# One planned order for scan, attention and gates of a gated mixer block, and a causal mask moved from TensorE to VectorE

## The chip, the cores and the metric

The kernel runs on one core of one Trainium2 chip. The metric is the device time of one execution in microseconds (us); lower is better. A core has a matrix engine (TensorE, in a profile PE, with its weight loads shown apart as PEld), a vector engine (VectorE, DVE), a scalar engine (ScalarE, ACT), a general engine (GpSimd, POOL) and a queue engine (SyncE, SP). Each works off its own list of instructions in order, and they wait for each other through semaphores.

## The reference

One layer of a streaming encoder on 512 tokens of width 1024: a half-step feed-forward, a mixer with two branches, and a second half-step feed-forward. The change lies in the mixer.

```python
h = rms_norm(x, mix_norm);  p = h @ w_in     # RWKV columns | FoX q, k, v, forget logits | gates A, B
y_A = rwkv7_mixer(token_shift(p_rwkv))       # 8 heads x 64, state S_t = S w_t + (S a_t) b_t' + v_t k_t'
y_B = forgetting_attention(q, k, v, log_f)   # 8 heads x 64, causal
x = x + (sigmoid(g_A) * y_A @ P_A + sigmoid(g_B) * y_B @ P_B) @ w_out

def one_block(i, q_i, c_i):                  # forgetting attention, 128 queries at a time
    s = einsum('bhqd,bhkd->bhqk', q_i, k) * scale + c_i[..., :, None] - cum[..., None, :]
    s = where(pos_k <= pos_q, s, -inf)       # the causal mask
    pr = softmax(s, axis=-1)
    return einsum('bhqk,bhkd->bhqd', pr, v)
```

## The kernel before

All activations lie transposed, 128 features on the partitions and 512 tokens along them. Products of weights and activations are made in three matmuls of split operands (`mm3`, lines 143 to 145): high by high, high by low, low by high. ScalarE rounds the high part of a weight column block (`whi`), VectorE subtracts it from the raw block (`wlo`), and eight groups of three matmuls then use it.

The stretch that the change touches begins when the first two pairs of attention heads have their queries and keys. Four kinds of work run beside each other in it:

- **The scan.** The recurrence of the first branch is worked in 16 chunks of 32 tokens (loop over `c`, lines 1522 to 1556). In each chunk TensorE makes `xps` (L1529), VectorE copies it to `Xs` (L1532), TensorE makes `ups` (L1536), ScalarE copies that into the chunk's operand `RD` with four copies (L1538, L1539), TensorE makes `sps` (the next state, L1544) and `yps` (the output, L1548), VectorE scales the state into the next chunk's `RD` with two instructions (L1551), and ScalarE copies the output (L1556). Each step waits for the one before it. Every second chunk, `stage` transposes the values and keys of two chunks (`vp`, `bp`, L1506 and L1509), and ScalarE copies them.
- **The attention.** Four pairs of heads, and in each three groups of query blocks: (0, 1), (2,), (3,). For each of the two heads `q`, TensorE writes logits into a bank `lp` with two matmuls for each query block (L1600, L1601), and a third adds the mask: the identity times `dmask`, which holds 0 and -1e30 (L1602, bf16, 128 by 128, on the diagonal block alone). VectorE takes the negated maximum (L1608), ScalarE the exponential with its sum (L1609), VectorE the reciprocal and the division (L1611, L1614), TensorE transposes (L1618), ScalarE copies (L1620), TensorE multiplies with the values (L1632), VectorE copies the result out (L1634).
- **The last key rows.** Query and key columns of head pairs 2 and 3 (`load_qk`): 24 matmuls each, and a norm of each row.
- **The gates.** Nine blocks of gate columns (`early`), 24 matmuls each, a product with the row norm (L1331), a tanh (L1334) and a store to memory.

What sets the order: each engine's list is written by a scheduler in the compiling layer, which goes by its own estimate of times, and the kernel ties places down with `tc.issue_after`. The list `holes` (line 1553) says after which scan step each group of three weight matmuls may stand: two groups behind `xps`, two behind `ups`, two or three behind `yps`. `AHEAD` (line 1560) says from which chunk on a head pair's operands are split. A class `Queued` can make an engine keep the order in which the source calls it (`written(True)`); it is on just before this stretch and again behind it, and off within it. The stores of the gates go out on SP's queue, between the loads of weights.

Of the kernel before, what the change touches and what calls it, by code (L numbers as in the profile page):

```python
# [18 lines left out]
P = 128  # L19
T = 512  # L20
# [30 lines left out]
def kernel(  # L51
# [67 lines left out]
    dmask = cp.tile([P, P], BF16, name="dmask")  # L119
# [50 lines left out]


# [222 lines left out]
    def masks():  # L394
# [7 lines left out]
        pool.affine_select(out=dmask[:], in_=dmask[:], compare_op=ALU.is_ge, fill=-1e30, base=0,  # L402
# [617 lines left out]
    with ExitStack() as mx:  # L1020
        rp = mx.enter_context(tc.tile_pool(name="rp", bufs=1))
        holes = []
# [303 lines left out]
        def gate(c0, m, g):  # L1326
            ps = bank("pgt")
            mms = mix.cols(ps[:], *load_w(win(c0 + m * P), KD, P), P, holes)

            def out(whole=True):  # L1330
                dve.tensor_tensor(g, ps[:], mix.rstd[:], op=ALU.mult)  # L1331
                if whole:
                    with tc.issue_after(qks["last"].ins):
                        qks["tanh"] = act.activation(g, g, AF.Tanh, scale=0.5)  # L1334
            return mms[-1], out


        def early(n):
            m = n + NP + 3
            g = xp.tile([P, T], F32, tag="acc", name="gs", bufs=2)  # L1340
            mm, scaled = gate(COL_GA, m, g[:])

            def out(whole=True):
                scaled(whole)
                if whole:
                    nc.sync.dma_start(gsave[m], g[:])
            return mm, out, g[:]


        class Rows(Columns):  # L1350
# [11 lines left out]
            def load(s, holes=()):  # L1362
                s.weights()
                mix.cols(s.ps[:], *s.w, P, holes)
# [35 lines left out]

        def load_qk(p, holes=()):
            rows = [Rows(p, n) for n in range(2)]
            for r in rows:
                r.load(holes)
                r.out()
            for r in rows:
                each([r], "square", "high", "sum")
            for r in rows:
                each([r], "log", "root", "scale")
            qks[p] = [r.o for r in rows]  # L1410
# [69 lines left out]
        each((b1,), "log", "root")  # L1480
        gate_out(True)
        last = dve.last
        written(False)
        with tc.issue_after(last.ins):
            b1.scale()
# [14 lines left out]
        def stage(c, behind=None):  # L1500
            late = ExitStack()
            if behind:
                late.enter_context(tc.issue_after(behind.ins))
# [18 lines left out]
        for c in range(NC):  # L1522
# [31 lines left out]
            if c % 2 == 0 and c + 2 < NC:  # L1554
                stage(c + 2, hy)
# [387 lines left out]
```

## Time and profile before

| what | us |
|---|---|
| median of three runs | 1104.52 (1104.48 to 1104.61) |
| the profiled execution | 1104.68 |
| its span, first to last instruction | 1103.0 |
| TensorE busy in the span | 1093.4 |
| the stretch of scan and attention | about 517 to 670 of the span |

A page of the profile gives busy time and counts by engine, the span in slices, the chain of work that ended last, and groups of instructions. A row of the timeline reads: start, duration, engine, line, operation, what is written `<-` what is read, shapes, how many; in brackets the idle time before it and what ended it. Matmuls overlap, so the pitch of a matmul, the start of the next minus its own start, is what it takes of TensorE's time; its shown duration is longer. The shown count of a matmul with plain 32-bit operands is twice that of the program.

### The profile page before, as it was taken

What the parts mean: (1) busy time and instruction counts of PE and PEld (TensorE: products, weight loads), DVE (VectorE), ACT (ScalarE), POOL (GpSimd) and SP (SyncE); (2) the same over time, 40 slices, a digit from 0 to 9 for tenths busy, and PEclk for the clock granted to TensorE, in tenths of its full rate; (3) what the DMA queues carried; (4) which work ended last, traced back from release to release, by engine and by line L of the source; (5) the groups of instructions that cost most, each with busy time, mean ns of one, the idle gap of its engine ahead of it and who ended that gap; (6) DMA issues with size and microseconds to landing.
All of it is one profiled execution on the core that took longest, in us unless ns stands there. A gap on an engine that the chain in (4) does not pass through costs nothing.

```text
span 1103.0 us, 16226 instructions
## 1 busy us (share of the span) xinstructions
PE 1093.4 (99%) x6082; PEld 893.1 (81%) x6082; DVE 837.1 (76%) x1130; ACT 670.4 (61%) x1046; POOL 207.0 (19%) x247
## 2 busy tenths in 40 slices
PE   9999999999999999999999999999999999999997
PEld 7888888888887888887777787888888888888886
DVE  7997676789766699788666667877697756789874
ACT  6765556675555756346787666633586555576554
POOL 1211211133204111401000011112311202115210
PEclk9999999999999999999999999999999999999999
DMA  8989887889926334445113234544968888869982
GB/s 226 249 176 236 195 181 190 192 153 193 241 77 195 94 104 117 115 134 139 45 40 96 86 100 144 175 135 141 285 153 190 195 215 172 183 159 204 236 189 77
DMA packets 140236, 177.09 MB, mean 161 GB/s; under 512 B 9726, under 2 KB 75838, under 8 KB 140158
## 3 DMA queue, kind: packets, MB, share of 16 engines
q0 software_dynamic: 32688, 68.30, 33.0%
q1 hardware_dynamic: 106734, 106.31, 31.4%
q10 hardware_dynamic: 736, 1.45, 0.3%
q8 instruction: 48, 0.79, 0.3%
q14 instruction: 30, 0.25, 0.1%
HBM read 163.51 MB, written 12.52 MB: 160 GB/s over the span
## 4 chain that ended last, share of the span: by engine, by line
PE 97%; ACT 1%; DMA 1%; DVE 1%; issue 0%; DVEq 0%; ACTq 0%
PE P L71 39%; PE P L143 5%; PE P L144 5%; PE P L145 5%; PE pgt L143 3%; PE pgt L145 2%; PE pgt L144 2%; PE pk L145 2%; PE pk L143 2%; PE pk L144 2%; PE ppj L71 2%; PE pb L71 1%; PE pa L71 1%; PE pq L143 1%; PE pw L144 1%; PE pw L143 1%
## 5 line engine op out<-in xcount | busy, mean ns | idle before, releaser
L135 ACT CAST whi<-raw 128x1024 fp32r<-128x1024 f32 (+3 forms) x57 | 55.3, 970 | 64.8 <-issue 19.3
L71 PE MATMUL P<-sraw,q 128*128 128x512 f32 x344 | 91.3, 389 | 0.0
L136 DVE TENSOR_TENSOR wlo<-raw,whi 128x1024 fp32r<-128x1024 f32 (+3 forms) x58 | 66.1, 1140 | 19.5 <-ACT whi L135 18.2
L71 PEld LDWEIGHTS P<-sraw,q 128*128 128x128 f32 x344 | 64.6, 188 | 13.4
L71 PE MATMUL P<-swhi,q 128*128 128x512 f32 x224 | 71.4, 390 | 0.0
L71 PE MATMUL P<-sraw,wxh 128*128 128x512 f32 x200 | 68.4, 394 | 0.0
L71 PE MATMUL P<-swhi,wxh 128*128 128x512 f32 x144 | 56.9, 395 | 0.0
L71 PE MATMUL P<-swhi,wxl 128*128 128x512 f32 x144 | 56.1, 390 | 0.0
L71 PE MATMUL P<-swlo,wxh 128*128 128x512 f32 x144 | 56.1, 389 | 0.0
L71 PE MATMUL P<-sraw,wxl 128*128 128x512 f32 x136 | 53.0, 390 | 0.0
L633 POOL DMA_DIRECT2D cb<-in_ffn_w_dram x20 | 24.1, 1203 | 149.6 <-DVE cd L71 85.2
L143 PE MATMUL pgt<-xh,whi 128*128 128x512 f32 x120 | 50.5, 421 | 0.0
L633 POOL DMA_DIRECT2D cd<-in_ffn_w_dram x24 | 29.5, 1230 | 104.2 <-DVE swlo L71 38.6
L71 PEld LDWEIGHTS P<-swhi,q 128*128 128x128 f32 x224 | 42.0, 188 | 8.7
L144 PE MATMUL pgt<-xl,whi 128*128 128x512 f32 x120 | 47.2, 393 | 0.0
L145 PE MATMUL pgt<-xh,wlo 128*128 128x512 f32 x120 | 47.1, 392 | 0.0
L71 PE MATMUL P<-swlo,q 128*128 128x512 f32 x112 | 43.6, 389 | 0.0
L71 PEld LDWEIGHTS P<-sraw,wxh 128*128 128x128 f32 x200 | 37.2, 188 | 7.3
L71 ACT CAST sraw<-cd 128x1024 fp32r<-128x1024 f32 x30 | 31.5, 1051 | 15.0 <-PE P L71 11.5
L71 DVE TENSOR_TENSOR swlo<-ca,swhi 128x1024 fp32r<-128x1024 f32 x24 | 29.2, 1222 | 14.0 <-ACT swhi L71 14.0
L71 DVE TENSOR_TENSOR swlo<-cc,swhi 128x1024 fp32r<-128x1024 f32 x20 | 24.5, 1225 | 18.9 <-ACT swhi L71 18.5
L71 DVE TENSOR_TENSOR u<-P,u 128x512 f32<-128x512 f32 x52 | 34.1, 684 | 5.8 <-ACT u L71 5.7
(624 smaller groups left out, 3371.3 us busy)
## 6 DMA issues: line engine op xcount, KB each, us to landing
raw<-in_w_in_dram SPq DMA_DIRECT2D x40, 512.0 KB
cc<-in_ffn_w_dram SPq DMA_DIRECT2D x36, 512.0 KB
cb<-in_ffn_w_dram POOLq DMA_DIRECT2D x36, 512.0 KB, 6.1
cb<-in_ffn_w_dram SPq DMA_DIRECT2D x32, 512.0 KB
cd<-in_ffn_w_dram POOLq DMA_DIRECT2D x32, 512.0 KB, 7.6
ca<-in_ffn_w_dram POOLq DMA_DIRECT2D x32, 512.0 KB, 7.2
ca<-in_ffn_w_dram SPq DMA_DIRECT2D x20, 512.0 KB
cd<-in_ffn_w_dram SPq DMA_DIRECT2D x18, 512.0 KB
```

What stands on the lines that cost most here:

```text
L71: q.last = do(*a, **kw)
L135: (hi_eng or act).copy(hi[:], raw[:])
L136: (eng or dve).tensor_tensor(lo[:], raw[:], hi[:].bitcast(F32), op=ALU.subtract)
L143: pe.matmul(ps, whi, xhi, start=first, stop=False, skip_group_check=onto)
L144: pe.matmul(ps, whi, xlo, start=False, stop=False, skip_group_check=onto)
L145: return pe.matmul(ps, wlo, xhi, start=False, stop=last, skip_group_check=onto)
L633: nc.gpsimd.dma_start(to, s.block(b, n, h), accum_op=ALU.add)
```

## The change

Everything of the stretch is entered into a `Plan`: an operation has an engine, a time in us, what it waits for, a rank, and the buffers it takes and frees. The plan then runs a clock of its own and always takes the operation that can start first, the lower rank first among equals; before an operation of rank over 0 on VectorE or ScalarE it looks whether a scan step could start within 1.32 times the operation's time, and takes that instead. It calls the operations in this order with the `Queued` wrapper on, so the written order is the order on TensorE, ScalarE and VectorE. `holes`, `AHEAD` and the waits between steps are gone. The wrapper stays on through the work behind the stretch, where its restart is dropped. The stores of these gates go out on POOL's queue. `dmask` grows to 128 by 512, with the mask in its last 128 columns, and is no operand of TensorE any more: VectorE adds it to the logits in the instruction that takes the maximum. The other splits, products and copies are the same.

```diff
-    dmask = cp.tile([P, P], BF16, name="dmask")
+    dmask = cp.tile([P, T], BF16, name="dmask")
...
+    class Plan:
...
+        def start(s, o):
+            to, now = o["engine"], s.idle.get(o["engine"], 0.0)
+            for d in o["deps"]:
+                if d["end"] is None:
+                    return None
+                by = d["engine"]
+                lag = 0.28 if by == "PE" else 0.15 if by == to else 0.2
+                now = max(now, d["end"] + (0.0 if by == to == "PE" else lag + 0.66 * (to == "PE")))
+            for name in set(o["takes"]):
...
+        def run(s):
+            todo = list(s.ops)
+            while todo:
+                at = {n: now for n, o in enumerate(todo) for now in [s.start(o)] if now is not None}
+                n = min(at, key=lambda n: (at[n], todo[n]["rank"], n))
+                o = todo[n]
+                if o["engine"] in ("DVE", "ACT") and o["rank"] > 0:
+                    until = at[n] + 1.32 * o["us"]
+                    n = next((m for m in at if todo[m]["engine"] == o["engine"] and todo[m]["rank"] == 0
+                              and at[m] < until), n)
...
+        SCAN, SIDE, NEXT, ROWS, FILL = range(5)
...
-            holes += [hx, hx, hu, hu, hy, hy] + [hy] * (c >= NC // 2)
...
+            e = op("PE", 0.58, on(product_x, c), *staged[c], *states.get(c, [begin]), rank=SCAN, takes=["pr"])
+            e = op("DVE", 0.22, copy_x, e, rank=SCAN, takes=["Xs"], frees=["pr"])
+            e = op("PE", 0.6, on(product_u, c), e, rank=SCAN, takes=["pr"], frees=["Xs"])
+            e = op("ACT", 1.07, on(copy_u, c), e, rank=SCAN, frees=["pr"])
...
-        AHEAD = (1, 6, 9, 12)
...
-                        pe.matmul(l, qb[q][:, bs], klc[q][:, 0:n], start=False, stop=False)
-                        pe.matmul(l[:, b * P:n], identb[:], dmask[:], start=False, stop=True)
+                    pe.matmul(l, qb[q][:, bs], klc[q][:, 0:n], start=False, stop=True)
...
-                        dve.tensor_reduce(mb, l, axis=AX.X, op=ALU.max, negate=True)
-                        act.activation(pt[:, at[b]:at[b] + n], l, AF.Exp, bias=mb, accum_out=mx[:, NB + b:NB + b + 1])
+                dve.tensor_tensor_reduce(l, l, dmask[:, T - (b + 1) * P:T], -1.0, 3e38, op0=ALU.add, op1=ALU.min,
+                                         accum_out=top)
...
+                act.activation(pts[:, q, n], s.lp[q][:, n], AF.Exp, bias=top, scale=-1.0, accum_out=sum_)
...
-                    nc.sync.dma_start(gsave[m], g[:])
+                nc.gpsimd.dma_start(gsave[m], g.t[:])
...
-        written(True)
-        pe.last, act.last, dve.last = gate_mm, filled, yl3
```

In the built program the new instruction on VectorE is two: one (`ISA lp,mx<-lp,dmask`) that adds, negates, writes the bank back and keeps the smallest value, and one (`ISA mx`) that writes this value out. TensorE's list behind the stretch is the same as before, row by row.

On TensorE, the first logits of head pair 2 (`kb`, `qa` and `klc`, `qb` are the split keys and queries, `RD` the scan's operands, `vp` and `bp` the scan's transposes) stood like this before:

```order
2620 L1600 MATMUL lp<-kb_5573,qa_5571 128x128
2621 L1601 MATMUL lp<-klc_3933,qb_4975 128x128
2622 L1602 LDWEIGHTS identb
2623 L1602 MATMUL lp<-dmask,identb 128x128
2624 L1600 MATMUL lp<-kb_5573,qa_5571 128x256
2625 L1601 MATMUL lp<-klc_3933,qb_4975 128x256
2626 L1602 LDWEIGHTS identb
2627 L1602 MATMUL lp<-dmask,identb 128x128
2628 L1544 MATMUL sps<-RD_4163,RD_4165 64x64 x8
```

and stand like this now:

```order
2470 L71 MATMUL vp<-ident,V_2815 64x128 x4
2471 L71 MATMUL lp<-kb_4959,qa_4957 128x128
2472 L71 MATMUL lp<-klc_3933,qb_4183 128x128
2473 L71 MATMUL lp<-kb_4959,qa_4957 128x256
2474 L71 MATMUL lp<-klc_3933,qb_4183 128x256
2475 L71 MATMUL lp<-kb_4959,qa_4957 128x384
2476 L71 MATMUL lp<-klc_3933,qb_4183 128x384
2477 L71 MATMUL bp<-ident,BK_2546 128x128
```

The two mask matmuls are gone, the next query block of the same head follows at once, and the group stands between the scan's transposes, about three chunks earlier in the scan than before (behind `sps` of chunk 6; before, ahead of `sps` of chunk 9).

On VectorE, between the state of one chunk and the `Xs` copy of the next (`pts` are the exponentials, `mx` the maxima and sums, `gs` a gate), chunk 7 stood like this before:

```order
589 L1551 TENSOR_TENSOR RD_4164<-sps,PC 64x4x64 x2
590 L136 TENSOR_TENSOR wlo<-raw,whi 128x1024
591 L1611 RECIPROCAL mx_4996<-mx_4996 128x1
592 L1532 COPY Xs<-xps 128x128
593 L1614 TENSOR_SCALAR pts<-pts,mx_4996 128x512
```

and chunk 4 stands like this now:

```order
586 L71 TENSOR_TENSOR RD_4156<-sps,PC 64x4x64 x2
587 L71 ISA lp,mx_4652<-lp,dmask 128x128
588 L71 ISA mx_4652 128x1
589 L71 ISA lp,mx_4652<-lp,dmask 128x256
590 L71 ISA mx_4652 128x1
591 L71 TENSOR_TENSOR wlo<-raw,whi 128x1024
592 L71 COPY Xs<-xps 128x128
```

In both a weight split stands right ahead of the scan's copy; now two masked maxima stand ahead of that. Such a split stands right ahead of `Xs` in five of the 16 chunks now (1, 4, 6, 13 and 14).

More of the change, by code (lines that the diff above doesn't have):

```diff
@@ L1399, in each @@
                     getattr(r, name)()
[L1401 to L1410, printed above, removed]
         qks = {}
@@ L1526, with product_x @@
+        def product_x(c):
+            Y["x"] = xps = pr.tile([P, 2, 64], F32, tag="b", name="xps")
             for p, q in heads()[::-1]:
                 o = (p // 2) * 64 + q * C
[L1528 to L1532 removed]
```

411 lines of the change are left out of this document (271 added, 140 removed).

## Prediction

> **What bounds the kernel now.** I read the page first, then one window over the stretch, then who waited for whom on TensorE there, then single rows of the timeline.
>
> ```profile
> span 1103.0 us, 16226 instructions
> PE 1093.4 (99%) x6082; PEld 893.1 (81%) x6082; DVE 837.1 (76%) x1130; ACT 670.4 (61%) x1046; POOL 207.0 (19%) x247
> PE 97%; ACT 1%; DMA 1%; DVE 1%; issue 0%; DVEq 0%; ACTq 0%
> ```
>
> The chain that ends last is TensorE for 97% of the span, so time is won or lost where TensorE does less, or waits more. The window over the stretch (columns: busy time and count by engine):
>
> ```profile
> 517.10:670.00 152.90, 151.76 (x1599) 117.91 (x1598) 104.00 (x230) 111.23 (x284) 7.86 (x15) 1.00 0.28 80
> ```
>
> TensorE is busy for 151.76 of 152.90 us; VectorE stands idle for 48.9 us of it and ScalarE for 41.7. All that TensorE waited there is 1.14 us, in three waits (waiter, releaser, total, times, longest):
>
> ```profile
> PE sps L1544 <- ACT RD L1539: 0.6, 1, 0.6
> PE lp L1618 <- DVE pts L1614: 0.3, 1, 0.3
> PE xps L1529 <- DVE RD L1551: 0.2, 1, 0.2
> ```
>
> So the order before leaves little to gain: a better order can give back 1.14 us here and no more. What is left to gain is work that TensorE no longer does.
>
> **Part 1: the mask leaves TensorE.** There are 32 of these matmuls:
>
> ```profile
> L1602 PE MATMUL lp<-dmask,identb x32: 229/229/233, 529.8 to 657.4; 128*128 128x128 bf16 x32
> ```
>
> Their price is a pitch, from one start to the next, and not the 229 ns of the row. Timeline of TensorE at the first logits of pair 2, at a mask followed by a weight matmul, and at a mask followed by the scan:
>
> ```profile
> 603.64 0.23 PE L1602 MATMUL lp<-dmask,identb 128*128 128x128 bf16 x1
> 603.68 0.36 PE L1600 MATMUL lp<-kb,qa 128*128 128x256 f32 x1
> 603.88 0.28 PE L1601 MATMUL lp<-klc,qb 128*128 128x256 f32 x1
> 604.00 0.23 PE L1602 MATMUL lp<-dmask,identb 128*128 128x128 bf16 x1
> 604.86 0.69 PE L1544 MATMUL sps<-RD,RD 128*64 128x64 f32 x16 [0.63 <-ACT RD L1539]
> ...
> 569.33 0.23 PE L1602 MATMUL lp<-dmask,identb 128*128 128x128 bf16 x1
> 569.37 0.48 PE L144 MATMUL pgt<-xl,whi 128*128 128x512 f32 x1
> 569.68 0.40 PE L145 MATMUL pgt<-xh,wlo 128*128 128x512 f32 x1
> 569.91 0.39 PE L143 MATMUL pgt<-xh,whi 128*128 128x512 f32 x1
> ...
> 635.81 0.23 PE L1602 MATMUL lp<-dmask,identb 128*128 128x128 bf16 x1
> 635.97 0.69 PE L1544 MATMUL sps<-RD,RD 128*64 128x64 f32 x16
> ```
>
> The mask itself takes 0.04 (603.64 to 603.68). The matmul of split operands behind it takes 0.08 more than its like: 0.20 (603.68 to 603.88) where the next one of the same width takes 0.12, and 0.31 (569.37 to 569.68) where a weight matmul takes 0.23 (569.68 to 569.91). In the order before, 14 masks have such a matmul behind them, 12 a scan or value product, 6 a transpose. Ahead of the scan a mask takes 0.16, but this 0.12 is no gain: a plain step into the scan has nearly the same toll, as these rows show, 0.32 (622.85 to 623.17) against 0.23 going in, and 0.34 (623.56 to 623.90) coming out.
>
> ```profile
> 622.85 0.40 PE L145 MATMUL pgt<-xh,wlo 128*128 128x512 f32 x1
> 623.17 0.46 PE L1536 MATMUL ups<-Xs,Tall 64*64 64x64 f32 x8
> 623.56 0.50 PE L143 MATMUL pgt<-xh,whi 128*128 128x512 f32 x1
> 623.90 0.40 PE L144 MATMUL pgt<-xl,whi 128*128 128x512 f32 x1
> ```
>
> Sum: 32 x 0.04 + 14 x 0.08 = 1.28 + 1.12 = 2.4 us less. The floor is the bare pitch, 1.3; the ceiling, with 0.05 for each of eight 128-wide matmuls ahead of a mask that might run closer to their width, 2.8. I take 2.4, since both of its terms stand in rows.
>
> **Part 2: the order.** The same products stand on TensorE in both kernels, so order costs only through tolls and waits. Tolls: counted in the two orders, narrow plain products are entered from weights, masks or transposes 52 times before and 54 times now (0.09 each), and left toward split-operand matmuls 42 and 34 times (0.11), toward transposes 10 and 20 times (about half as dear): 0.2 for the entries, 0.9 against the exits, 0.5 for the transposes. That is zero to within 0.2 us.
>
> Waits: 1.14 us could go. The longest, 0.63 at 604.86, came because ScalarE made a weight high part ahead of the scan's copies:
>
> ```profile
> 602.67 1.05 ACT L135 CAST whi<-raw 128x1024 fp32r<-128x1024 f32 x1
> 603.74 0.25 ACT L1538 COPY RD<-ups 32x128 f32<-32x128 f32 x1
> ```
>
> The plan's rule (a scan step goes first if it could start within 1.32 operations) is aimed at this, and behind every `ups` TensorE now has over 2.0 us of other work by the pitches above; the copies need 0.3 and then 1.06. What could be late next is the other side: behind `xps` the cover falls from at least 1.58 before to 0.9 to 1.0 in two chunks (11 and 14). How much the copy of `xps` needs when VectorE is free or busy is seen in chunk 7:
>
> ```profile
> 577.92 0.45 PE L1529 MATMUL xps<-RD,G 128*32 128x64 f32 x16 [0.20 <-DVE RD L1551]
> 578.29 0.50 PE L143 MATMUL pgt<-xh,whi 128*128 128x512 f32 x1
> 579.89 0.45 PE L1536 MATMUL ups<-Xs,Tall 64*64 64x64 f32 x8
> ...
> 577.80 1.22 DVE L136 TENSOR_TENSOR wlo<-raw,whi 128x1024 fp32r<-128x1024 f32 x1
> 578.94 0.15 DVE L1611 RECIPROCAL mx<-mx 128x1 f32<-128x1 f32 x1
> 579.13 0.29 DVE L1532 COPY Xs<-xps 128x128 f32<-128x128 f32 x1
> ```
>
> Behind a weight split the copy began 0.84 after the next matmul's start at 578.29 and `ups` followed 0.47 after its end: 1.60 in all, with a cover of 1.60 and no wait that the profile shows. With VectorE free some 0.75 less is needed. I take half of the 1.14 as gained, 0.6: between 1.1 gained and, if the thin covers fail (below), 1.0 lost.
>
> The operands' splits, the transposes of chunk 0 (which move into the stretch from weight matmuls just ahead of it, where TensorE did not wait either), and the stores on POOL's queue I cost at nothing. What hides the stores: a store is wanted only when its buffer is used again two gates later, over 10 us. Behind them on POOL stand the loads of gates for the last products; 33 weight matmuls (33 x 0.23 = 7.6 us) now end the stretch, which cover them.
>
> **Part 3: the mask on VectorE.** 32 maxima, and each gets a second input, a written bank and a second instruction that reads its result out. The rows of before (busy, mean ns), and the nearest ones for two inputs:
>
> ```profile
> L1608 DVE TENSOR_REDUCE mx<-lp 128x1 f32<-128x512 f32 x8 | 5.4, 688 | 3.2 <-PE lp L1602 3.0
> L1608 DVE TENSOR_REDUCE mx<-lp 128x1 f32<-128x384 f32 x8 | 4.3, 555 | 5.0 <-PE lp L1602 5.0
> L1608 DVE TENSOR_REDUCE mx<-lp 128x1 f32<-128x256 f32 x8 | 3.4, 423 | 1.5 <-ACT pts L1609 1.3
> L1608 DVE TENSOR_REDUCE mx<-lp 128x1 f32<-128x128 f32 x8 | 2.3, 284 | 0.6 <-PE lp L1602 0.6
> L1331 DVE TENSOR_TENSOR gs<-pgt,rstd 128x512 f32<-128x512 f32 x8 | 5.5, 690 | 1.3 <-PE pgt L145 1.2
> L1218 DVE TENSOR_TENSOR_SCAN G<-cmask,G 128x512 f32<-128x512 f32 x2 | 2.4, 1221 | 0.0
> ...
> L1609 ACT ACTIVATION_READ_ACCUMULATOR pts<-lp,mx x32: 192/193/212, 533.3 to 659.2; 128x1 f32 x32
> ...
> 679.54 0.75 DVE L71 SCALAR_TENSOR_TENSOR V<-V,par,G 128x512 f32<-128x512 f32 x1
> ```
>
> Now they cost 5.4 + 4.3 + 3.4 + 2.3 = 15.4 us. Low end: an elementwise product of a bank and a tile takes 690 ns for 512, as the maximum does, so nothing is added. High end: the rate of the running scan, 1221 ns, and a read-out as dear as ScalarE's 193: (1221 - 688) x 20 (the 32 maxima are 20 widths of 512) + 32 x 193 = 10.7 + 6.2 = 16.9 us. I take the elementwise rate, because the new instruction has the same kind of inputs, with some 0.1 for the read-out: 3 us on VectorE, against 48.9 idle. It lies beside TensorE's work, so 0 in the sum.
>
> [...]
>
> **The sum.** 2.4 + 0.6 = 3.0 us less: 1104.68 - 3.0 = 1101.7 for the profiled execution. The median of the runs lies 0.16 below that execution, so 1101.5.
>
> **The rivals.**
>
> *New waits give it back, no real change.* Of the five chunks where a weight split stands right ahead of `Xs`, two have covers below the 1.60 of chunk 7: 1.24 (chunk 4) and 1.01 (chunk 14). That is 0.4 + 0.6 = 1.0 us of new waits, and the old 1.14 may stay under other names: 1104.5 - 2.4 + 1.0 = 1103.1. For it: one strict order on three engines lets no late step be passed. Against it: VectorE's share is 68%, and the split is seldom the last to come.
>
> *Only the bare pitch goes.* The 0.08 behind a mask could belong to whatever follows, and the waits stay: 1104.5 - 1.3 = 1103.2.
>
> *Slower: the masked maximum runs at the scan's rate.* Then two maxima ahead of `Xs`, as in chunk 4, add (384/512) x 0.53 + 2 x 0.19 = 0.8 us to it, three (chunks 0 and 8) 1.4, and every softmax gets longer by as much ahead of its transposes. With covers of 0.9 to 2.1 behind `xps`, I reckon 0.35 us of wait for each of 16 chunk steps and 0.1 for each of 24 transposes: 5.6 + 2.4 = 8.0, so 1104.5 - 3.0 + 8.0 = 1109.5; it decides from 3.0 us of new waits on. For it: the one scan row. Against it: the elementwise rows.
>
> **How the numbers follow.** A change under 0.2%, 2.2 us, is about what a measurement of this kernel cannot tell from none. The forecast, 1101.5, has 0.58; its own range is 1099.7 (2.8 of masks, 1.1 of waits, and 0.9 of matmul tolls that I set to zero) to 1102.3. The two cases of 1103 together have 0.25. The slow maximum has 0.12, and other slips on the slow side (a store or a load late in a queue) 0.05. So faster 0.58, same 0.25, slower 0.17. The range, 1099.6 to 1105.6, holds the forecast and both cases near 1103 and the mild end of the slow ones, and leaves the rest of these out.
>
> **What would show it.** In the profile after: no `dmask` on TensorE and 64 fewer instructions; TensorE's waits in the stretch under 1 us in all (right), or a list of `ups <- DVE Xs` and `lp <- DVE pts` of over 3 us (wrong); the stretch from the last `bonesr` sum of pair 1 to the first `yc` 3 us shorter, once the 0.9 us of chunk 0's transposes are taken off; the masked maximum of 512 at about 0.7 us (right) or 1.2 (the slow rival). I am wrong if the three written orders, which cannot let a later step pass, make TensorE stand still in places that no cover counted here shows.

## The result and the profile after

The changed kernel takes 1101.46 us, the median of 8 runs (1100.88 to 1101.77); the kernel before took 1104.62 in the 8 runs beside it. The ratio is 0.997, with a 95% interval of 0.996 to 0.9981. The forecast was 1101.5, in a range of 1099.6 to 1105.6.

The profiled execution after took 1101.58 us. Its page, in the same three lines as the page of before:

```profile
span 1099.8 us, 16207 instructions
PE 1090.9 (99%) x6050; PEld 889.6 (81%) x6050; DVE 839.4 (76%) x1162; ACT 669.3 (61%) x1046; POOL 212.0 (19%) x255
PE 97%; ACT 1%; DVE 1%; DMA 0%; issue 0%; DVEq 0%; ACTq 0%
```

The chain still ends on TensorE for 97% of the span, with 32 matmuls fewer in the trace and 2.5 us less busy time.

The signs that the prediction named are there: `dmask` is gone from TensorE (32 matmuls and 32 weight loads fewer in the page), and the stretch from the last `bonesr` sum of pair 1 to the first `yc`, the one of the prediction, is 2.92 us shorter (152.90 to 149.98), 3.8 once the 0.9 of chunk 0's transposes are taken off, where 3 was forecast:

```profile
517.40:667.38 149.98, 149.62 (x1575) 114.55 (x1574) 106.00 (x260) 114.48 (x295) 12.66 (x23) 1.00 0.31 91
```

TensorE's idle time in it fell from 1.14 to 0.36. To compare orders I take a longer stretch than the prediction did, one that begins and ends at the same two matmuls in every kernel: from the last `gp` matmul (behind it the orders begin to differ) to the first `yc`. The window over it, in the kernel before and then in the kernel after (length, then busy time and count of TensorE, its weight loads, VectorE, ScalarE and GpSimd, then clock, share of the DMA engines and GB/s):

```profile
461.20:670.01 208.81, 207.67 (x1853) 163.76 (x1850) 149.18 (x321) 140.81 (x330) 18.10 (x34) 1.00 0.34 95
```

```profile
461.88:667.39 205.51, 204.67 (x1821) 159.66 (x1818) 150.77 (x351) 139.60 (x330) 22.97 (x42) 1.00 0.36 102
```

The stretch became 3.30 us shorter: TensorE is busy for 3.00 less (207.67 to 204.67), and idle for 0.30 less (1.14 to 0.84). What remains of its waits, in the list of who waited for whom in the changed kernel's stretch:

```profile
PE pq L71 <- DVE l L71: 0.5, 1, 0.5
PE pgt L71 <- DVE gs L71: 0.2, 1, 0.2
```

None of the three waits of before is in it, and no `ups <- DVE Xs`. The first of the two that are listed is new, and lies ahead of the prediction's stretch, where the chunk-0 transposes are gone:

```profile
506.51 0.69 DVE L71 TENSOR_TENSOR l<-qsq,h 128x512 fp32r<-128x512 f32 x1
507.26 0.50 PE L71 MATMUL pq<-l,bonesr 128*128 128x512 f32 x1 [0.48 <-DVE l L71]
```

On TensorE nothing else differs up to there: it comes to the sum of `h` just ahead of this one 0.97 earlier in the stretch than before (44.50 us into it for 45.47), VectorE to `l` only 0.40 earlier (44.63 for 45.03).

Outside the stretch the two profiled executions differ by 0.68 lost ahead of it and 0.56 gained behind it. Neither can be put down to the change. Ahead of the stretch the orders are the same, and every other profile taken in this study begins it 0.3 to 1.1 later than that one profile of before (461.54 to 462.27, against 461.20), the three whose TensorE was slower throughout (below) left out. Behind it, the profile of before shows a late landing of the load of `lgsave`, and a run with the old order, described below as the one with the mask on VectorE, has the load leave at the same time and no wait. First the rows of before:

```profile
667.98 1.32 SPq L1669 DMA_DIRECT2D G<-lgsave  x1
675.21 0.62 ACT L71 CAST gl<-G 96x512 fp32r<-96x512 f32 x1 [1.22 <-DMA G<-lgsave]
```

And of the old order with the mask on VectorE, where both casts follow each other at once:

```profile
668.21 0.42 SPq L1669 DMA_DIRECT2D G<-lgsave  x1
673.62 1.14 ACT L71 CAST gl<-G 96x512 fp32r<-96x512 f32 x2
```

So the comparisons below go by the stretch and by the medians, and leave head and tail out. Each stretch is one profiled execution. In the batches of the experiments the kernel before had medians of 1104.19 to 1104.31, not 1104.62; each ratio is to the kernel before of the same batch.

The masked maximum, grouped by form, in the changed kernel (busy, mean ns, idle before):

```profile
L71 DVE CUSTOM_DVE_ANT_0 lp<-lp,dmask 128x512 f32<-128x512 f32 x8 | 5.6, 699 | 2.9 <-PE lp L71 2.8
L71 DVE CUSTOM_DVE_ANT_0 lp<-lp,dmask 128x384 f32<-128x384 f32 x8 | 4.6, 580 | 0.4 <-PE lp L71 0.4
L71 DVE DVE_READ_ACCUMULATOR2_ANT mx<- 128x1 f32 x32 | 4.3, 134 | 0.1
L71 DVE CUSTOM_DVE_ANT_0 lp<-lp,dmask 128x256 f32<-128x256 f32 x8 | 3.5, 432 | 0.3
L71 DVE CUSTOM_DVE_ANT_0 lp<-lp,dmask 128x128 f32<-128x128 f32 x8 | 2.4, 300 | 1.2 <-PE lp L71 0.9
```

It takes 699 ns for a full bank, the elementwise rate (690) and not that of the running scan (1221), and 16.1 us in all against 15.4 before. The read-out takes 134 ns.

Chunk 4, one of the two that the prediction feared, in the changed kernel, with two masked maxima and a weight split ahead of `Xs`:

```profile
557.60 0.43 DVE L71 CUSTOM_DVE_ANT_0 lp<-lp,dmask 128x256 f32<-128x256 f32 x1
557.95 0.14 DVE L71 DVE_READ_ACCUMULATOR2_ANT mx<- 128x1 f32 x1
557.95 1.22 DVE L71 TENSOR_TENSOR wlo<-raw,whi 128x1024 fp32r<-128x1024 f32 x1
558.42 0.44 PE L71 MATMUL xps<-RD,G 128*32 128x64 f32 x16
559.08 0.28 DVE L71 COPY Xs<-xps 128x128 f32<-128x128 f32 x1
560.04 0.46 PE L71 MATMUL ups<-Xs,Tall 64*64 64x64 f32 x8
```

`Xs` ended at 559.36, and `ups` came 0.68 later, when its place in the order came: no wait. The read-out and the split both start at 557.95, so the read-out holds up nothing behind it here. Of the 32 read-outs, 13 have the next instruction start with them; behind 12 others it starts 0.09 to 0.21 later.

### The profile page after: what moved, and what is told of

Same layout as the page of the kernel before. It is cut to its first block, busy times and chain, and to the rows that moved or that the text cites. A ratio compares the mean times of both kernels' runs of the same rounds, so it can differ in the third digit from the quotient of the medians.

```text
span 1099.8 us, 16207 instructions
## 1 busy us (share of the span) xinstructions
PE 1090.9 (99%) x6050; PEld 889.6 (81%) x6050; DVE 839.4 (76%) x1162; ACT 669.3 (61%) x1046; POOL 212.0 (19%) x255
## 3 DMA queue, kind: packets, MB, share of 16 engines
q10 hardware_dynamic: 736, 1.45, 0.3%
## 4 chain that ended last, share of the span: by engine, by line
PE 97%; ACT 1%; DVE 1%; DMA 0%; issue 0%; DVEq 0%; ACTq 0%
PE P L71 39%; PE P L144 5%; PE P L145 5%; PE P L143 5%; PE pgt L71 5%; PE lp L71 3%; PE pq L71 2%; PE pk L145 2%; PE ppj L71 2%; PE pk L143 2%; PE pk L144 2%; PE pb L71 2%; PE pa L71 1%; PE pw L144 1%; PE pw L145 1%; PE pw L143 1%
## 5 line engine op out<-in xcount | busy, mean ns | idle before, releaser
L135 ACT CAST whi<-raw 128x1024 fp32r<-128x1024 f32 (+3 forms) x43 | 41.1, 956 | 65.4 <-issue 19.3
L136 DVE TENSOR_TENSOR wlo<-raw,whi 128x1024 fp32r<-128x1024 f32 (+3 forms) x44 | 49.6, 1127 | 17.8 <-ACT whi L135 16.6
L543 POOL DMA_DIRECT2D ca<-in_ffn_w_dram x16 | 19.3, 1205 | 96.4 <-DVE swlo L71 66.4
L143 PE MATMUL pk<-xh,whi 128*128 128x512 f32 x96 | 37.8, 394 | 0.0
L145 PE MATMUL pk<-xh,wlo 128*128 128x512 f32 x96 | 37.5, 391 | 0.0
```

The source lines that it names most:

```text
L135: (hi_eng or act).copy(hi[:], raw[:])
L136: (eng or dve).tensor_tensor(lo[:], raw[:], hi[:].bitcast(F32), op=ALU.subtract)
L143: pe.matmul(ps, whi, xhi, start=first, stop=False, skip_group_check=onto)
L145: return pe.matmul(ps, wlo, xhi, start=False, stop=last, skip_group_check=onto)
L543: nc.gpsimd.dma_start(s.sum[g], src, accum_op=ALU.add)
```

## The experiments

The question is where the 3.3 us come from: from the mask, from the order, or from both together. Four kernels ask it first. "Old order" is that of the kernel before.

**The mask back on TensorE, in the new order.** The plan's operations and their times stay as they are; the exponential's `scale=-1.0` goes again.

```diff
-                    pe.matmul(l, qb[q][:, bs], klc[q][:, 0:n], start=False, stop=True)
+                    pe.matmul(l, qb[q][:, bs], klc[q][:, 0:n], start=False, stop=False)
+                    pe.matmul(l[:, b * P:n], identb[:], dmask[:, T - P:T], start=False, stop=True)
...
-                dve.tensor_tensor_reduce(l, l, dmask[:, T - (b + 1) * P:T], -1.0, 3e38, op0=ALU.add, op1=ALU.min,
-                                         accum_out=top)
+                dve.tensor_reduce(top, l, axis=AX.X, op=ALU.max, negate=True)
```

> The changed kernel with its plan and order as they are, but each query block's logits again end with the mask matmul on TensorE, and VectorE takes the plain maximum. In this order 23 of the 32 masks have a matmul of split operands behind them (12 logits, 10 weights, 1 sum), where before it was 14. If a mask costs 0.04 and 0.08 more in the split-operand matmul behind it: 32 x 0.04 + 23 x 0.08 = 3.1 us more than 1101.5, so 1104.6, and the order by itself would have given nothing. If only the bare pitch counts: 1.3 more, 1102.8. If the gain came from the order alone: 1101.5.

Measured: 1104.59 us, ratio to before 1.0002 (0.9994 to 1.0011). The window over its stretch:

```profile
461.56:670.01 208.45, 207.76 (x1853) 161.04 (x1850) 148.67 (x319) 139.91 (x330) 22.97 (x42) 1.00 0.35 99
```

With the same order, the 32 mask matmuls cost 207.76 - 204.67 = 3.09 us of busy time (3.49 between its median and that of the changed kernel with its stores on SP's queue, below, which ran in the same batch), where 32 x 0.04 + 23 x 0.08 gives 3.1. So the price of a mask depends on what stands behind it, as the prediction had it. And the new order alone, the mask left where it was, is worth 0.36 in the stretch, all of it idle time (1.14 to 0.69), and nothing that the medians show (1104.59 against 1104.30; the profiled execution, 1104.14, was the fastest of eleven).

**The mask on VectorE, in the old order.** `dmask` is widened and the exponential gets its `scale=-1.0`, as in the changed kernel.

```diff
-                        pe.matmul(l, qb[q][:, bs], klc[q][:, 0:n], start=False, stop=False)
-                        pe.matmul(l[:, b * P:n], identb[:], dmask[:], start=False, stop=True)
+                        pe.matmul(l, qb[q][:, bs], klc[q][:, 0:n], start=False, stop=True)
...
-                        dve.tensor_reduce(mb, l, axis=AX.X, op=ALU.max, negate=True)
+                        dve.tensor_tensor_reduce(l, l, dmask[:, T - n:T], -1.0, 3e38, op0=ALU.add, op1=ALU.min,
+                                                 accum_out=mb)
```

> The kernel before, scheduled as before, with the mask taken from TensorE and added by VectorE with the maximum. If the masks cost 0.04 each and 0.08 behind 14 of them: 2.4 us less than 1104.6, so 1102.2, with TensorE's waits in the stretch near the old 1.1 us. If only the bare pitch counts: 1103.3. If the old order cannot bear longer maxima on VectorE, new waits of several us behind Xs and pts: 1104 or more.

Measured: 1104.25 us, ratio 0.9997 (0.9988 to 1.0006): no gain. The window over its stretch:

```profile
461.69:670.26 208.57, 205.38 (x1821) 162.62 (x1818) 150.25 (x353) 141.10 (x330) 18.23 (x34) 1.00 0.34 95
```

Its waits there (waiter, releaser, total, times, longest):

```profile
PE sps L1544 <- ACT RD L1539: 1.5, 2, 1.0
PE xps L1529 <- DVE RD L1551: 1.4, 2, 1.1
```

And the two longest of them in its timeline, each with what stood ahead on the other engine:

```profile
576.84 0.75 DVE L1394 SCALAR_TENSOR_TENSOR qk<-qk,par,qrn 128x512 f32<-128x512 f32 x1
577.51 0.85 DVE L1551 TENSOR_TENSOR RD<-sps,PC 64x256 f32<-64x256 f32 x2
578.51 0.45 PE L1529 MATMUL xps<-RD,G 128*32 128x64 f32 x16 [1.12 <-DVE RD L1551]
...
603.55 1.04 ACT L135 CAST whi<-raw 128x1024 fp32r<-128x1024 f32 x1
604.62 0.25 ACT L1538 COPY RD<-ups 32x128 f32<-32x128 f32 x1
605.73 0.69 PE L1544 MATMUL sps<-RD,RD 128*64 128x64 f32 x16 [0.98 <-ACT RD L1539]
```

TensorE's busy time fell by 207.67 - 205.38 = 2.29, close to the 2.4 forecast for the masks. But its idle time grew from 1.14 to 3.19, and took nearly all of it back. The place at 605.73 is the one that the prediction showed at 604.86, with the same cast of a weight part ahead of the same copies: the wait there went from 0.63 to 0.98. At 578.51 the kernel before waited 0.20, at 577.92, with other work ahead on VectorE:

```profile
576.53 0.48 DVE L1614 TENSOR_SCALAR pts<-pts,mx 128x512 f32<-128x512 f32 x1
576.92 0.85 DVE L1551 TENSOR_TENSOR RD<-sps,PC 64x256 f32<-64x256 f32 x2
```

Counted from the start of the stretch, `RD` ended at about the same time in both (116.57 before, 116.67 here), but TensorE stood at `xps` 0.82 earlier (115.70 for 116.52). So this wait grew since TensorE came sooner. At 605.73 TensorE came at the same time as before (143.06 for 143.03), and the copies were later, behind the earlier waits.

**No mask at all, in the new order.** The mask is left out, and the exponential's `scale=-1.0` with it.

```diff
-                dve.tensor_tensor_reduce(l, l, dmask[:, T - (b + 1) * P:T], -1.0, 3e38, op0=ALU.add, op1=ALU.min,
-                                         accum_out=top)
+                dve.tensor_reduce(top, l, axis=AX.X, op=ALU.max, negate=True)
```

> The changed kernel with the plain maximum and no mask anywhere: the causal mask is left out, so the attention sees later keys. VectorE loses the second input, the write-back and the read-out: 5.0 us of its work by the rows of the changed kernel (20.4 against 15.4). If VectorE's part is hidden: 1101.5, within 0.3. If the longer maxima cost TensorE waits of which only few are listed: 0.5 to 2 us less, 1099.5 to 1101.0.

Measured: 1101.13 us (0.997, 0.9958 to 0.9982). Its window:

```profile
461.83:667.31 205.48, 204.63 (x1821) 159.66 (x1818) 148.43 (x319) 139.63 (x330) 23.20 (x42) 1.00 0.35 101
```

The stretch is 0.03 shorter than with the masked maximum. VectorE's busy time differs by 150.77 - 148.43 = 2.3 us, and TensorE sees none of it.

**The stores of the gates back on SP's queue.**

```diff
-                nc.gpsimd.dma_start(gsave[m], g.t[:])
+                nc.sync.dma_start(gsave[m], g.t[:])
```

> The changed kernel with the stores of the gates back on SP's queue. TensorE waited 0.6 us less behind the stretch, where the load of lgsave left at 659.9 instead of 668.0. If that is due to the scan's earlier end (659.6 instead of 667.7), which frees the tile it writes: 1101.5, the load at about 664, behind the last store, and no wait on pg. If it is due to SP's queue being free of stores: 1102.1, the load late and the wait of 0.2 to 0.6 on pg back. A raw weight load queued behind a store would show as a wait of ScalarE on whi, and only beyond some 4 us of delay on TensorE.

Measured: 1101.1 us (0.997, 0.9959 to 0.9982), a stretch of 205.49 and no wait on `pg`. The queue of the stores changes nothing that the stretch or the median shows. Of the two causes that this expectation offered for the tail, the second is refuted here, and the first by the old order with the mask on VectorE, where the scan ends at 667.92 and there is no wait either.

**What made the waits in the old order?** Longer maxima on VectorE, or a TensorE that has less to do and so stands sooner at a step that is not ready? The old order without any mask tells these apart: the mask matmul goes, and the maximum stays plain.

```diff
-                        pe.matmul(l, qb[q][:, bs], klc[q][:, 0:n], start=False, stop=False)
-                        pe.matmul(l[:, b * P:n], identb[:], dmask[:], start=False, stop=True)
+                        pe.matmul(l, qb[q][:, bs], klc[q][:, 0:n], start=False, stop=True)
```

> The kernel before, scheduled as before, without the causal mask anywhere: the mask matmuls are left out and the maximum stays the plain one, so the attention sees later keys. With the mask on VectorE in the old order the stretch from the last gp matmul to the first yc took 208.57 us, with waits of 2.9, against 208.81 and 1.1 before. If those waits came from the longer maxima on VectorE: they go back to about 1.1 here, the stretch takes 206.8 and the kernel 1102.4. If they came because TensorE, with less to do, reaches the scan's steps sooner than ScalarE and VectorE, whose lists put other work ahead of the scan's copies: waits of 2 to 3 us again, a stretch of 208 to 208.6, and 1104.

Measured: 1104.0 us (0.9998, 0.9988 to 1.0007). Its window, and behind it its waits:

```profile
462.27:670.57 208.30, 205.47 (x1822) 162.62 (x1819) 149.16 (x321) 140.88 (x330) 18.33 (x34) 1.00 0.34 95
```

```profile
PE sps L1544 <- ACT RD L1539: 1.4, 2, 1.0
PE xps L1529 <- DVE RD L1551: 1.3, 2, 1.0
```

The same waits stand at the same steps, 2.83 us idle in all, without a single longer maximum. The orders of TensorE, ScalarE and VectorE in the two traces are the same row by row, so the masked maximum is cleared; in the old order the saved TensorE time itself turns into waits. One reservation: the old order is made by the compiling layer's scheduler, which places some rows otherwise once the masks are gone: in the stretch 20 of 1814 on TensorE, 15 of 330 on ScalarE and 14 of 320 on VectorE, the product ahead of `RD` at 577.51 among them. No run holds it fixed. For the longest wait the rows above show TensorE's earlier arrival as the cause; how much the moved rows add to the others is not told apart. The executions of this kernel lie 1.3 us apart (1103.28 to 1104.59), and the profiled one, 1104.54, is among the longest.

**Which part of the plan protects the scan?** Two kernels each take away one of its rules.

```diff
-                    until = at[n] + 1.32 * o["us"]
+                    until = at[n] + 0.0 * o["us"]
```

> The changed kernel, but its plan holds no operation back for a scan step that could start soon (the 1.32 is 0): the orders of TensorE, ScalarE and VectorE all change. By counted tolls the order costs TensorE 0.4 us more. If the look-ahead is what makes the removed masks pay: casts of weight parts and long products stand ahead of the scan's copies again, waits on RD and Xs of 1.5 to 3 us, 1103 to 1105. If the covers on TensorE do it (1.1 to 2.6 behind xps, 1.4 and more behind ups, about as before): waits under 1 us, 1102.

Measured: 1103.35 us (0.9991, 0.9982 to 1.0001). Its window:

```profile
461.65:669.35 207.70, 206.08 (x1821) 159.88 (x1818) 150.19 (x351) 138.70 (x330) 22.59 (x42) 1.00 0.33 94
```

The stretch is 2.19 longer than in the changed kernel, with 1.62 idle. So without the look-ahead about two thirds of the gain is gone. The time is that of the expectation's first branch, but neither branch describes how: idle time grew by 0.78 only, and busy time by 1.41, of which 0.4 were counted as tolls. A part of that may be waits that do not show, since matmuls overlap: a row is 0.39 long at a pitch of 0.23, so a delay of up to 0.16 appears as busy. The second run with doubled maxima below shows that such waits exist; for this run the split stays open.

```diff
-                now = max(now, d["end"] + (0.0 if by == to == "PE" else lag + 0.66 * (to == "PE")))
+                now = max(now, d["end"] + (0.0 if by == to == "PE" else lag + 0.0 * (to == "PE")))
```

> The changed kernel, but its plan gives TensorE no margin of 0.66 us after the work of another engine: TensorE's covers shrink to 0.7 to 1.6 behind xps (0.9 to 2.1 in the changed kernel), 1.7 and more behind ups, and to between 0.1 and 1.5 for half of the value products and 1.0 to 2.4 for four groups of transposes late in the stretch. Tolls by count 0.4 us less. In the changed kernel Xs begins 0.31 behind the last xps matmul and takes 0.29, so 0.8 is needed there, and 1.6 behind ups. If waits follow from the covers: some 0.3 at ups, 3 at value products and 3 to 6 at transposes, 1107 to 1111. If the covers count for little because other work stands behind: 1101 to 1102.

Measured: 1115.08 us (1.01, 1.0085 to 1.0115), slower than any branch. Windows around its worst waits, cut where the granted clock changes (columns as above; the clock is the third number from the end):

```profile
628.37:631.78 3.41, 1.14 (x20) 0.82 (x19) 2.48 (x6) 1.70 (x5) 1.06 (x2) 1.00 0.60 167
631.78:635.19 3.41, 2.95 (x18) 2.40 (x18) 0.94 (x3) 1.88 (x5) 0.00 (x0) 0.50 1.02 326
635.19:638.61 3.42, 1.45 (x18) 0.85 (x16) 1.73 (x4) 3.33 (x5) 0.00 (x0) 1.00 0.13 34
638.61:648.85 10.24, 7.72 (x21) 6.00 (x22) 8.97 (x24) 6.17 (x15) 2.69 (x5) 0.50 0.43 125
```

Rows of TensorE's timeline there, the two waits and two weight matmuls behind them:

```profile
631.08 0.52 PE L71 MATMUL lp<-ident,pts 128*128 128x128 f32 x3 [2.09 <-DVE pts L71]
640.60 0.47 PE L71 MATMUL lp<-kb,qa 128*128 128x128 f32 x1 [3.89 <-DVE qa L71]
644.44 0.63 PE L71 MATMUL pgt<-xl,whi 128*128 128x512 f32 x1
644.87 0.63 PE L71 MATMUL pgt<-xh,wlo 128*128 128x512 f32 x1
```

The stretch is 13.2 us longer, of which 7.6 are idle time that the windows show (0.84 to 8.42). The rest, 5.6, is busy time, most of it from a lower clock: behind each wait the granted clock is 0.50, for 3.41 and for 10.24 us, and a weight matmul has a pitch of 0.43 (644.44 to 644.87) where it has 0.23. TensorE did 2.95 + 7.72 us of work at that clock; if half of it is what the clock cost (an estimate from the 0.50), that is 5.3. This was in no expectation. The changes of the clock lie 3.41, 3.42 and 10.24 us apart, and the 3.41 and 3.42 us ahead of the two falls were not idle throughout: TensorE was busy for 1.14 and 1.45 us of them. What makes the clock fall, and what brings it back, this run does not show. The longest wait, on the operands `qa` of the last head pair, was also one whose cover I had not counted.

**How much can VectorE carry?** The prediction's slow rival priced some 17 us more on VectorE at 8 us. Doing each masked maximum twice tests that price: first with its read-out going into a new small tile that nothing reads, then as before.

```diff
+                    s.pair.junk = tp.tile([P, 1], F32, tag="junk", name="junk", bufs=2)
...
+                dve.tensor_tensor_reduce(l, l, dmask[:, T - (b + 1) * P:T], 1.0, -3e38, op0=ALU.add, op1=ALU.max,
+                                         accum_out=s.pair.junk[:])
                 dve.tensor_tensor_reduce(l, l, dmask[:, T - (b + 1) * P:T], -1.0, 3e38, op0=ALU.add, op1=ALU.min,
...
+                if s.pair.p == 0 and s.bl == (3,):
+                    dve.tensor_tensor_reduce(pts[:, q, :], pts[:, q, :], pts[:, q, :], 0.5, -3e38, op0=ALU.add,
+                                             op1=ALU.max, accum_out=s.pair.junk[:])
```

> The changed kernel with its plan and order as they are, but VectorE takes each masked maximum twice: 20.4 us more of its work, about what the slow rival of the prediction gave it (16.9 more), and nothing in the plan knows of it. By the working of that rival (0.35 for each chunk and 0.1 for each group of transposes) 8 us more or a fifth above: 1109 to 1111. If TensorE's covers hide it: 1101.5 to 1103. In the last query block of the first pair VectorE also adds the exponentials to themselves and halves them, two 32-bit tiles in SBUF with an accumulator, 512 wide: 0.7 us for each if it runs at the rate of the masked maximum, 1.2 to 1.3 at half rate.

Measured: 1117.67 us (1.0122, 1.0107 to 1.0137). The stretch took 6.25 more, but the rest of the kernel, which is the same program, took 9.9 more as well: TensorE's pitch was longer far from the stretch. (Over all its 128x512 matmuls outside the stretch the mean pitch is 0.232 for 0.229; the median is 0.229 for 0.227, not the 0.231 of the next expectations.) So this run did not answer its question. It did answer the other one; the two forms in its groups:

```profile
L71 DVE CUSTOM_DVE_ANT_0 lp<-lp,dmask 128x512 f32<-128x512 f32 x16 | 11.2, 703 | 1.5 <-PE lp L71 1.2
L71 DVE CUSTOM_DVE_ANT_0 pts<-pts 128x512 f32<-128x512 f32 x2 | 1.4, 693 | 0.1
```

With two 32-bit inputs in SBUF (here the same tile twice) the instruction took 693 ns, no more than with one input in a bank (703). Half that rate would make about 1.24 us (an estimate from the 703 ns of this run for 512 columns and its 299 for 128), and that does not show. The rows are of a custom operation, so the run tells of this operation only.

Again without the new tile, the first read-out going into the column of the sums:

```diff
+                dve.tensor_tensor_reduce(l, l, dmask[:, T - (b + 1) * P:T], 1.0, -3e38, op0=ALU.add, op1=ALU.max,
+                                         accum_out=s.of(q, b)[2])
```

> The doubled masked maximum once more, without a new tile: its read-out goes into the column that the sum of the exponentials overwrites later. In the run with a new tile the stretch took 6.3 us more than in the changed kernel, but TensorE was also slower by 1.1% far from the stretch (pitch of weight matmuls 0.231 for 0.227), 9.8 us in all outside it. If that slower pitch came with the new tile and not with the doubled maximum: TensorE at 0.227 again outside the stretch, and inside only the new waits, some 4 us by the list of waits, so 1105 to 1106. If the doubled instruction causes it: 1117 again.

Measured: 1106.1 us (1.0016, 1.0007 to 1.0026). The window, and the longest of its waits in the timeline:

```profile
461.88:672.10 210.22, 206.01 (x1822) 159.44 (x1818) 166.57 (x415) 139.98 (x330) 22.68 (x42) 1.00 0.35 99
```

```profile
588.93 0.46 PE L71 MATMUL ups<-Xs,Tall 64*64 64x64 f32 x8 [0.95 <-DVE Xs L71]
```

VectorE does 166.57 - 150.77 = 15.8 us more, and the stretch takes 4.7 more: 0.30 of each us. The rival's working gave 0.47 (8.0 of 16.9). TensorE's order is the same as in the changed kernel, and yet its busy time rose by 1.34, so delays too short to show as idle do count: matched row by row, 4.2 of the 4.7 lie at steps that show a wait in either trace, where the pitch grew by 0.07 to 0.16 more than the new wait shows, and 0.5 at steps that show none. Some 16 us more on VectorE are enough to undo the whole gain; the 2.3 that the change brings are not felt.

**Why was TensorE slower throughout?** A kernel that differs from the changed one in the unread tile and the four memsets that fill it:

```diff
+                    s.pair.junk = tp.tile([P, 1], F32, tag="junk", name="junk", bufs=2)
+                    pool.memset(s.pair.junk[:], 0.0)
```

> The changed kernel with one more small tile (128 by 1, two buffers) in the pool of the maxima, filled once for each head pair by GpSimd and never read; the tiles behind it lie 64 bytes further on in SBUF, all orders are the same. If the place of the tiles sets TensorE's pitch: 0.231 outside the stretch, about 11 to 12 us more than the changed kernel, 1112 to 1114. If not: 1101.5.

Measured: 1111.63 us (1.0067, 1.0053 to 1.0081), with a stretch of 205.57, as in the changed kernel. A window far ahead of the stretch, in the changed kernel and then here:

```profile
100.00:300.00 200.00, 200.00 (x917) 166.10 (x916) 154.90 (x163) 120.17 (x149) 49.57 (x42) 1.00 0.89 194
```

```profile
100.00:300.00 200.00, 200.00 (x903) 163.54 (x902) 153.44 (x161) 117.63 (x147) 48.76 (x42) 1.00 0.87 190
```

In the same 200 us, at the same granted clock and with no idle time, TensorE does 903 matmuls instead of 917. The memsets take 0.1 us each, between 3.8 and 5.0 us, and the first doubled run, which has the tile but not the memsets, has the same mean pitch of 0.232; so what is left is the tile itself, behind which other tiles lie 64 bytes further on. Not every matmul is slower: outside the stretch `P<-sraw,q` has a median pitch of 0.234 for 0.227, and `pk<-xh,whi` 0.227 for 0.226. That fits a cause in the place of certain tiles, but no run shows which.

**Can the order give more?** A plan that takes a matmul of the same kind as the last one where it can, so that fewer tolls are paid, and with the margin at 0.75 for 0.66 (`kind` is "thin" for the scan and the value products, "turn" for transposes, "wide" for the rest):

```diff
+                if o["engine"] == "PE" and o["rank"] > 0:
+                    like = [m for m in at if todo[m]["engine"] == "PE" and at[m] <= at[n] + 0.1]
+                    if last == "thin":
+                        n = min(like, key=lambda m: ("thin", "turn", "wide").index(todo[m]["kind"]))
+                    elif o["kind"] == "thin" and at[n] < o.setdefault("ripe", at[n]) + 2.0:
+                        n = next((m for m in like if todo[m]["kind"] != "thin"), n)
```

> The changed kernel with a plan that looks at the kind of the last matmul: behind narrow products it takes another narrow one, then a transpose, ahead of a wide one, if one is ready within 0.1 us; a value product that stands behind a wide matmul may be held back up to 2 us; and the margin is 0.75 instead of 0.66. By count narrow products are entered 48 times instead of 54, and the tolls sum to 9.3 us instead of 10.5; the thinnest cover behind xps is 1.64 instead of 0.9, behind ups 1.98 instead of 2.04. If tolls are real and the covers hold: 1.2 us less, 1100.2 to 1100.4, TensorE's waits in the stretch no more than now. If tolls are only shares of the same pipeline time: 1101.5. If holding back value products makes new waits (behind them stand the buffers of logits): 1102 or more.

Measured: 1101.28 us (0.9972, 0.9962 to 0.9983), which cannot be told from the changed kernel. Its window, and its new waits in the timeline:

```profile
461.97:667.13 205.16, 203.71 (x1821) 160.19 (x1818) 149.71 (x351) 139.15 (x330) 21.87 (x41) 1.00 0.33 94
```

```profile
620.26 0.63 PE L71 MATMUL bp<-ident,BK 128*128 128x128 f32 x4 [0.53 <-DVE RD L71]
621.95 0.45 PE L71 MATMUL xps<-RD,G 128*32 128x64 f32 x16 [0.36 <-ACT RD L71]
```

Busy time fell by 0.96, near the 1.2 of counted tolls, which speaks for tolls being real (the order and the margin changed with them, so it is not shown apart); idle time rose by 0.61 at two steps that I had not counted covers for (the buffer of `bp`, and the staging copies ahead of `xps`). What was left is 0.35.

**The same plan, with the tiles at multiples of 128 bytes** (the unread tile with three buffers).

> The plan that groups narrow products, and the small unread tile of the run before with three buffers instead of two: the tiles behind the pool of the maxima lie 96 bytes further on than in the changed kernel, at multiples of 128 bytes, where they were 32 past a multiple in the changed kernel and 96 past it in the run that took 10 us more. If it is the place within 128 bytes that counts, and a multiple is no worse than 32 past it: a pitch of 0.227 or less outside the stretch, 1101.3 or less. If any other place than the present one costs: 0.231 and 1111.

Measured: 1112.8 us (1.0077, 1.006 to 1.0094), a mean pitch of 0.232 outside the stretch, and 205.1 in it. So it is not that a multiple of 128 is the good place. Both places tried, 64 and 96 bytes further on, are worse than the one the kernel has; which tile it is, and why, stays open.

## Why the prediction was right

**The sum.** Forecast 3.0 us less (2.4 for masks, 0.6 for waits), measured 3.30 in the stretch (3.00 busy, 0.30 idle) and 3.16 between the medians. The total is better than its terms: busy time fell by 0.6 more than forecast, idle time by 0.3 less, and the two errors partly cancel.

**Part 1, the masks.** The price of a mask (0.04, and 0.08 where split operands stand behind it) held in two orders: 2.29 of busy time where the count gave 2.4, and 3.09 where it gave 3.1. The bare pitch of 1.3 is excluded. The ceiling of 2.8 was set for the old order; in the new one more masks would have had split operands behind them.

**Part 2, the order.** I set the tolls of the order to zero. With the mask on TensorE in both orders that came out (0.09 more busy time); with the mask on VectorE the new order has 0.71 less (205.38 to 204.67). How much of that is tolls and how much delays at the old order's waits that do not show as idle is not told apart. The waits: in the prediction's own stretch they fell by 0.78 (1.14 to 0.36), where I took 0.6. But chunk 0's transposes, which I cost at nothing because TensorE did not wait where they stood, left a new wait of 0.48 at 507.26, so over the longer stretch only 0.30 is gained.

The thin covers made no wait: in chunk 14, where I counted 1.01, `Xs` ended 0.60 behind the last `xps` matmul by the rows, and `ups` came 0.57 later. The rival of new waits was priced too high for this order: it read the 1.60 of chunk 7 as what a copy behind a weight split needs, but 1.60 was the cover, and the 0.47 between `Xs` and `ups` came from TensorE's order, not from a need. Where `ups` did wait for `Xs`, at 588.93 in the doubled run, it started 0.15 behind its end; and in chunk 14 the copy did not have to wait for the split.

But one sentence of the prediction was wrong: that a better order can give back 1.14 "here and no more". It treats the two parts as terms to be added. The runs show that they are not:

| stretch, us (idle) | old order | new order |
|---|---|---|
| mask on TensorE | 208.81 (1.14) | 208.45 (0.69) |
| mask on VectorE | 208.57 (3.19) | 205.51 (0.84) |

The mask alone gives 0.24, the order alone 0.36, both 3.30. (The first two are smaller than the differences between executions of one kernel; by the medians each is nothing.) In the old order the time that TensorE is spared comes back as waits on the scan's copies; the new order's worth is that it lets the 2.3 to 3.1 us through. That was luck in part: my number came out since I priced the masks as if no wait would follow, which is true of the new order only. The first rival, that new waits give the gain back, names what happens in the old order.

**Part 3, VectorE.** 699 ns and 134 ns, as taken (690 and 100); 2.3 us more of busy time where I reckoned 3; nothing of it on TensorE's path. The slow rival needed the rate of the running scan, which the instruction does not have, and its price was about half too high again (0.47 for 0.30 per us).

**The stores** cost nothing that shows on either queue, as forecast.

## What to carry to other kernels

Here TensorE is busy for 99%, a chain with other engines in it runs beside the bulk, and time taken off TensorE counted only where the steps of that chain were ready in time. In such a kernel, change the load and the order together, and test each alone before saying which one paid. A list of small waits is not the ceiling of what an order is worth (here 1.14 us were listed and 3.06 came with the order once the mask was gone), for the list changes as soon as the engine has less to do (1.14 to 3.19 in the old order); and delays shorter than the overlap of two matmuls (0.16 here) do not stand in it at all. Work that moves out from ahead of a step can uncover a wait there, even where there was none before (0.48 at 507.26). Price a small matmul by the pitch of itself and of the one behind it, in the place where it stands.

## What was not expected of the hardware

- One more small tile that nothing reads, with the tiles behind it 64 or 96 bytes further on in SBUF, came with a slower TensorE in all three kernels that had it: a mean pitch of 0.232 instead of 0.229 for 128x512 matmuls outside the stretch, at the same granted clock, and in the one that is otherwise the changed kernel 10.2 us more (1111.63 against 1101.46), three times what the change gained. The stretch itself was not affected (205.57 against 205.51). That the place of the tiles is the cause is the nearest reading, and not shown further.
- In the plan without the margin idle time came with a price beyond itself: around waits of 2.09 and 3.89 us the granted clock was 0.50 from 631.78 to 635.19 and from 638.61 to 648.85, with TensorE busy for 1.14 and 1.45 us of the 3.41 and 3.42 ahead of each fall. Of the 13.2 us lost in that run 5.6 were busy time, most of it matmuls at a pitch of up to 0.43 instead of 0.23.
- The read-out of the accumulator, 134 ns as shown, costs less than that in many places: 13 of 32 overlap the next instruction of VectorE from its start, as at 557.95 in the rows above, and 20.4 us of doubled instructions added 15.8 of busy time.
